# Attention states relative to each chunk's middle, with one decayed key and query, and forget gates of latents and context as 512-column products

## The chip, the cores and the metric

The kernel runs on one core of a Trainium2 chip. The metric is the time of one execution on the device in microseconds; lower is better. The core's engines are TensorE (PE, with its loads of stationary operands as PEld), VectorE (DVE), ScalarE (ACT), GpSimd (POOL) and SyncE (SP, which issues most DMAs). Each takes its instructions in program order and waits on semaphores for the others.

## The reference

One block over 256 latent tokens with 256 context tokens, width 1024: modulated norm, one combined projection, two mixers (a bidirectional gated linear recurrence in chunks of 64 with a state from the context, and a spatial MLP), projections and gates, and then a mixture of 32 experts. The change is in the recurrence and the projections of its forget gates.

```python
def decay(f_logit, lb):
    f = lb + (1.0 - lb) * jax.nn.sigmoid(f_logit.astype(jnp.float32))
    return heads(1.0 - f), heads(jnp.log(f))
...
def step(s, xs):                       # one chunk of 64 tokens, per head and direction
    qc, kc, vc, gc = xs
    b = jnp.cumsum(gc, axis=1)
    b_ref = b[:, A_CHUNK // 2 - 1:A_CHUNK // 2]
    b_end = b[:, -1]
    scores = jnp.einsum('bthd,bshd->bhts', qc * jnp.exp(b - b_ref), kc * jnp.exp(b_ref - b))
    scores = jnp.where(lower, scores, 0.0)
    o = (jnp.einsum('bhts,bshv->bthv', scores, vc)
         + jnp.einsum('bthd,bhdv->bthv', qc * jnp.exp(b), s))
    s = (jnp.exp(b_end)[..., None] * s
         + jnp.einsum('bshd,bshv->bhdv', kc * jnp.exp(b_end[:, None] - b), vc))
    return s, o
...
def final_state(k, v, logf):           # over the context, gives the first s
    tail = lax.cumsum(logf, axis=1, reverse=True) - logf
    return jnp.einsum('bshd,bshv->bhdv', k * jnp.exp(tail), v)
```

## The kernel before

Every dense product is computed as three products of rounded parts: `split` (L263) has ACT round a tile to `hi` and DVE subtract to get `lo`, for the weights as `ghi` and `glo`, for the modulated activations as `hh` and `hl`. A `Granule` is 1024 x 256 weights, fetched by SP into a ring of three slots; `dense` (L330) goes over it in two halves of four k-tiles, each with its own `ghi` and `glo`.

Phase one: the modulation weights and the modulated activations come in four quarters, together with pair 0's values and forget gates (24 to 84 us). Then a loop over j = 0 to 4 with eight heads in pairs. Iteration j computes the dense projections of pair j (`pair_dense`: d0 values, d1 query, d2 output gate, d3 and d4 the two forget gates; in iteration 4 gates of the second mixer instead) and the attention of the pair before: for its two heads x and y step 0 is `decays`, 1 `states`, 2 `output`, 3 `finish`. The string `ORDER` (L1056) gives the order in which the program is written, "x0 d0 y0 m0 d1 x1 m1 d2 x2 y1 x3 m2 d3 y2 m3 y3 d4"; a scheduler then orders each engine's instructions. m0 to m3 are parts of the weighted sums of later modulation weights: POOL multiplies 128x2048 (L215), adds halves (L216, L221); DVE does the other part (L228). In the profile pairs 1 to 4 stand at 84 to 157, 157 to 228, 228 to 298 and 298 to 345 us (the iteration in which their attention is done for the pair before).

`decays` takes the sigmoid of both forget gates (k, latents and context side by side): DVE maps it to f (L442), ACT takes the logarithm, POOL makes 1 - f (L446). DVE's scans (L453) run along tokens, per chunk in the latents (bl) and over the whole context (cu), per direction. d1 is bl relative to the chunk's middle (L466), d2 the chunk's end relative to bl (L467). Five exponentials on ACT follow, and five products: on DVE q and k for the scores (L475, L476), k for the states (L477), q for the output (L479), and on POOL the context's k (L478).

`states`: scores on PE (L496), k transposed (L506) and copied by ACT or DVE (L507), the chunks' state updates U and the context's state (L515, L518; in banks `ua` and `ub`). `output`: per direction three steps S[next] = S * decay of the chunk + U on DVE (L528, L530), then o on PE (L535, L539). `finish` normalises and gates.

After the loop: the second mixer, gates, branch projections, `w_out`, the router (345 to about 500 us), and the experts, whose 12 MB each are fetched through slots made of whatever phase one no longer needs (`slots`, L774 and after), the tags d0 to d3 and big1 of the pool `consts` among them.

Of the kernel before, what the change touches and what calls it, by code (L numbers as in the profile page):

```python
# [31 lines left out]
def kernel(  # L32
# [406 lines left out]
    def decays(hd, k, q):  # L439

        for dr in range(2):
            ve.tensor_scalar(k[:, dr], k[:, dr], omlb[dr][:, hd:hd + 1], lb[dr][:, hd:hd + 1], op0=OP.mult, op1=OP.add)  # L442
# [2 lines left out]
        tc.keep_in_program_order(sc.activation(lf, k, AF.Ln))
        gp.tensor_scalar(k, k, -1.0, 1.0, op0=OP.mult, op1=OP.add)  # L446
# [3 lines left out]
        def scan(o, dst, src, so, m, rev):  # L450
            st = -1 if rev else 1
            e = T - 1 if rev else 0
            ve.tensor_tensor_scan(view(dst, o + e, [[st, T]]), m, view(src, so + e, [[st, T]]),  # L453
                                  0.0, op0=OP.mult, op1=OP.add)

        chunks, whole = reset, view(reset, 1, [[0, T]])
        scan(0, bl, lf, 0, chunks, False)
        scan(T, bl, lf, 2 * T, chunks, True)
        scan(0, cu, lf, T, whole, True)
        scan(T, cu, lf, 3 * T, whole, False)  # L460
# [631 lines left out]
```

## Time and profile before

| what | value |
|---|---|
| median of 3 runs | 1448.78 us (1447.9 to 1449.63) |
| profiled execution: own time, span of its trace | 1449.62 us, 1447.4 us |
| granted clock of PE, mean | 0.98 |
| busy share of the span: PE, DVE, ACT, POOL | 93%, 44%, 21%, 11% |
| DMA | 487.41 MB, mean 337 GB/s |

The shares are means over stages that differ: the first third is phase one, the rest the experts. Matmuls are pipelined, and a row's duration is longer than the step to the next one; the pitch of a stretch is its length over its matmuls. An idle time in brackets names what ended it.

### The profile page before, as it was taken

The page shows a single profiled execution, that of the slowest core. Times are in us where ns is not written, and L with a number is a line of the kernel's source. Part 1 is how long each engine was busy: PE and PEld are TensorE (multiplying, and loading weights), DVE is VectorE, ACT ScalarE, POOL GpSimd, SP SyncE. Part 2 cuts the span into 40 slices and gives each one's busy share as a digit, 9 for nine tenths or more (in the row PEclk, how much of TensorE's full clock was granted, in tenths as well). Part 3 has the DMA queues.
Part 4 walks back from the last instruction along what each step waited for, and adds up shares of the span by engine and source line. Part 5 has one row for each costly group of instructions (what it writes and reads, how often), then busy time and mean ns, then how long its engine had stood idle before and what let it go on. Part 6 is the DMA issues. An engine that isn't in the chain of part 4 may idle for free. (4 is left out here: it accounts for less than half of the span.)

```text
span 1447.4 us, 19272 instructions
## 1 busy us (share of the span) xinstructions
PE 1344.3 (93%) x8190; PEld 750.8 (52%) x8190; DVE 643.5 (44%) x1106; ACT 307.7 (21%) x493; POOL 161.6 (11%) x107
## 2 busy tenths in 40 slices
PE   6979898989999999999999999989999899999996
PEld 4979788878999843333333333323333233232322
DVE  5498888888769623223223222222232232322214
ACT  2363444454444310100100101000000000000001
POOL 3054323240046000000000000000000000000001
PEclk8989999999999999999999999999999999999999
DMA  9535252534894899999999999999999999999994
GB/s 334 189 116 196 96 198 67 203 117 155 287 263 173 315 422 392 423 425 424 423 426 425 426 422 423 426 428 422 425 424 424 426 426 424 423 425 426 425 424 183
DMA packets 109909, 487.41 MB, mean 337 GB/s; under 512 B 6614, under 2 KB 65115, under 8 KB 77435
## 3 DMA queue, kind: packets, MB, share of 16 engines
q1 hardware_dynamic: 108970, 483.38, 83.5%
q0 software_dynamic: 848, 2.75, 0.6%
q8 instruction: 66, 1.08, 0.3%
q14 instruction: 25, 0.20, 0.0%
HBM read 485.06 MB, written 1.05 MB: 336 GB/s over the span
## 5 line engine op out<-in xcount | busy, mean ns | idle before, releaser
L829 PE MATMUL gate<-w,xT 128*64 128x512 f32 x1024 | 270.9, 608 | 18.5 <-DMA w<-in_w_dram 18.1
L829 PE MATMUL lin<-w,xT 128*64 128x512 f32 x1024 | 264.0, 594 | 0.0
L866 PE MATMUL py<-w,hT 128*64 128x512 f32 x992 | 223.1, 595 | 22.1 <-DMA w<-in_w_dram 22.0
L885 DVE SCALAR_TENSOR_TENSOR acc<-sc,wts,acc 128x512 f32<-128x512 f32 x122 | 86.0, 747 | 214.0 <-PE sc L882 214.0
L345 PE MATMUL acc<-hh,ghi 128*128 128x256 f32 x576 | 167.5, 291 | 11.5 <-ACT iv L427 11.5
L345 PE MATMUL acc<-hh,glo 128*128 128x256 f32 x576 | 165.8, 288 | 10.3 <-DVE glo L266 10.3
L345 PE MATMUL acc<-hl,ghi 128*128 128x256 f32 x576 | 165.3, 287 | 0.0
L266 DVE TENSOR_TENSOR glo<-w,ghi 128x1024 fp32r<-128x1024 f32 (+1 forms) x99 | 141.8, 1439 | 49.7 <-ACT ghi L265 49.3
L829 PEld LDWEIGHTS lin<-w,xT 128*64 128x64 f32 x1024 | 73.5, 138 | 147.9 <-issue 147.9
L866 PEld LDWEIGHTS py<-w,hT 128*64 128x64 f32 x992 | 69.1, 136 | 156.0 <-issue 111.7
L829 PEld LDWEIGHTS gate<-w,xT 128*64 128x64 f32 x1024 | 63.1, 137 | 158.2 <-issue 104.9
L265 ACT ACTIVATE ghi<-w 128x1024 fp32r<-128x1024 f32 (+1 forms) x102 | 102.3, 1007 | 144.7 <-PE acc L345 110.1
L345 PEld LDWEIGHTS acc<-hh,ghi 128*128 128x128 f32 x576 | 111.4, 193 | 12.7 <-ACT iv L427 11.9
L345 PEld LDWEIGHTS acc<-hh,glo 128*128 128x128 f32 x576 | 111.1, 193 | 11.7 <-DVE glo L266 11.5
L345 PEld LDWEIGHTS acc<-hl,ghi 128*128 128x128 f32 x576 | 111.5, 194 | 0.7 <-issue 0.7
L869 DVE TENSOR_TENSOR y<-py,g2h 128x512 f32<-128x512 f32 x31 | 21.4, 692 | 183.9 <-PE py L866 183.9
L964 POOL DMA_DIRECT2D bc<-in_final_g_dram x1 | 0.6, 557 | 892.4 <-DMA w<-in_w_dram 892.4
L804 ACT ACTIVATE xT<-misc,sh,a 128x128 f32<-128x128 f32 (+1 forms) x68 | 30.7, 452 | 284.3 <-DVE xT L806 284.3
L806 DVE TENSOR_SCALAR xT<-misc,a,sh 128x128 f32<-128x128 f32 (+1 forms) x68 | 27.3, 401 | 136.0 <-PE misc L800 125.4
L345 PE MATMUL acc<-ghi,hh 128*128 128x256 f32 x256 | 73.9, 291 | 13.7 <-DVE og L416 6.3
L836 DVE TENSOR_SCALAR g<-gate 128x512 f32<-128x512 f32 x32 | 22.1, 692 | 137.2 <-PE gate L829 137.2
L800 PEld LDWEIGHTS misc<-p,acc 128*128 128x128 f32 x544 | 66.6, 196 | 26.6 <-issue 26.0
(325 smaller groups left out, 1696.9 us busy)
## 6 DMA issues: line engine op xcount, KB each, us to landing
w<-in_w_dram SPq DMA_DIRECT2D x127, 2048.0 KB, 27.1
w<-in_w_dram SPq DMA_DIRECT2D x130, 1024.0 KB, 27.1
w<-in_w_in_dram SPq DMA_DIRECT2D x33, 1024.0 KB, 5.5
w<-in_w_mod_dram SPq DMA_DIRECT2D x24, 1024.0 KB, 5.6
w<-in_w_branch_b_dram SPq DMA_DIRECT2D x4, 1024.0 KB
w<-in_w_branch_a_dram SPq DMA_DIRECT2D x4, 1024.0 KB, 12.7
w<-in_w_out_dram SPq DMA_DIRECT2D x4, 1024.0 KB, 10.6
w<-in_w_in_dram SPq DMA_DIRECT2D x12, 256.0 KB, 8.6
```

Of the source, the lines that this page charges most:

```text
L265: sc.activation(hi, src, AF.Copy)
L266: eng.tensor_sub(lo, src, hi)
L345: te.matmul(o, l, r, start=opens and kt == 0 and n == 0, stop=kt == KT - 1 and n == 2, skip_group_check=True)
L800: te.matmul(pg[:, k], view(x1, tt * D + kt // 2 * 256 + kt % 2, [[2, P]]), tok[:, tt], start=tt == 0, stop=tt == 1)
L804: sc.activation(xT[:, kt], pg[:, k], AF.Identity, bias=sh2[:, kt:kt + 1], scale=a2[:, kt:kt + 1])
L806: ve.tensor_scalar(xT[:, kt], pg[:, k], a2[:, kt:kt + 1], sh2[:, kt:kt + 1], op0=OP.mult, op1=OP.add)
L829: te.matmul(zz[n][h * C:(h + 1) * C], xT[:, kt], w[:, 0, n * D + h * 512:n * D + (h + 1) * 512], start=False, stop=kt == KT - 1, skip_grou ...
L836: ve.tensor_scalar(g, zz[0], 7.0, None, op0=OP.min)
L866: te.matmul(py[h * C:(h + 1) * C], hT2[:, kt % 4, (kt // 4) * C:(kt // 4) * C + C], w[:, k, h * 512:(h + 1) * 512], start=False, stop=kt = ...
L869: ve.tensor_mul(y, py, g2h)
L885: ve.scalar_tensor_tensor(acc[:, tt, s], pcs[h], wcol[tt], old[:, tt, s], op0=OP.mult, op1=OP.add)
L964: gp.dma_start(fgbc, bcast(final_g, D))
```

## The change

The states are kept relative to the middle of each chunk. The key for the scores, k * exp(b_ref - b), is then also that of the state updates, and the query q * exp(b - b_ref) also that of the output; d2, two exponentials, and two DVE products a head are left out. What remains of the decays are factors per chunk and channel: `w` (128x16), copied on POOL from bl and d1 and exponentiated. A step of the state is an addition (S + U) and a scaling by two such factors, on DVE for one direction and on POOL for the other; the context's state is scaled when ACT copies it.

The logarithm takes scale and bias, so that L442 goes (ACT's logarithm is four 128x512 of two heads instead of two 128x1024); products with 1 - f become scalar_tensor_tensor with the negated factor; POOL's 1 - f covers the context alone; the scan over the context starts one token late with a memset column instead of a subtraction on POOL (L462).

Latents and context lie side by side in one buffer (`both`), and a forget granule is 48 products of 512 columns instead of 96 of 256. The two buffers take the whole tags d2 and d3 (two units each), so the experts' slots are d0, d1 and big1 with one unit, d2 and d3 with two, and two instead of three in `ringc`.

```diff
-    hT = [(consts.tile([P, KT, T], F32R, name="hh0", tag="d3"), consts.tile([P, KT, T], F32R, name="hl0", tag="d2")),
-          (mid.tile([P, KT, T], F32R, name="hh1"), mid.tile([P, KT, T], F32R, name="hl1"))]
+    both = (consts.tile([P, KT, 2, T], F32R, name="hh", tag="d3"), consts.tile([P, KT, 2, T], F32R, name="hl", tag="d2"))
+    hT = [[t[:, :, a] for t in both] for a in range(2)]
+    both = [t.rearrange("p k a t -> p k (a t)") for t in both]
...
-        return [(pps[ct][:, a], ct, hT[a], a == 0) for ct in range(2) for a in range(2)]
+        return [(pps[ct].rearrange("p a t -> p (a t)"), ct, both, True) for ct in range(2)]
...
-        for dr in range(2):
-            ve.tensor_scalar(k[:, dr], k[:, dr], omlb[dr][:, hd:hd + 1], lb[dr][:, hd:hd + 1], op0=OP.mult, op1=OP.add)
...
-        tc.keep_in_program_order(sc.activation(lf, k, AF.Ln))
-        gp.tensor_scalar(k, k, -1.0, 1.0, op0=OP.mult, op1=OP.add)
+        for dr in range(2):
+            tc.keep_in_program_order(sc.activation(lf[:, dr], k[:, dr], AF.Ln, scale=omlb[dr][:, col], bias=lb[dr][:, col]))
+        kl, kc = k[:, :, 0:T], k[:, :, T:2 * T]
+        gp.tensor_scalar(kc, kc, -1.0, None, op0=OP.add)
...
+        gp.memset(view(cu, T - 1, [[1, 2]]), 0.0)
...
-        gp.tensor_sub(cu, cu, e2)
...
-        ve.tensor_sub(view(d2, 0, [[T, 2], [64, 4], [1, 64]]), view(bl, 63, [[T - 63, 2], [64, 4], [0, 64]]), bl4)
+        w = wk.tile([P, 2, 2, 4], F32, name="w")
+        gp.tensor_copy(w[:, 0], view(bl, 31, [[T + 1, 2], [64, 4]]))
+        gp.tensor_copy(w[:, 1], view(d1, 63, [[T - 63, 2], [64, 4]]))
         sc.activation(e1, d1, AF.Exp)
         sc.activation(e2, d1, AF.Exp, scale=-1.0)
-        sc.activation(bl, bl, AF.Exp)
-        sc.activation(d2, d2, AF.Exp)
         sc.activation(cu, cu, AF.Exp)
-        qb = q[:, None, :].to_broadcast([P, 2, T])
-        kl, kc = k[:, :, 0:T], k[:, :, T:2 * T]
-        ve.tensor_mul(e1, e1, qb)
-        ve.tensor_mul(e2, e2, kl)
-        ve.tensor_mul(d2, d2, kl)
+        sc.activation(w, w, AF.Exp)
+        for dr in range(2):
+            ve.scalar_tensor_tensor(e1[:, dr], e1[:, dr], nomlb[dr][:, col], q, op0=OP.mult, op1=OP.mult)
+        ve.scalar_tensor_tensor(e2, kl, -1.0, e2, op0=OP.add, op1=OP.mult)
         gp.tensor_mul(cu, cu, kc)
-        ve.tensor_mul(d1, bl, qb)
-        return e1, e2, bl, d1, d2, cu
+        return e1, e2, cu, w
...
-            for a, src in ((0, kb), (1, kc)):
+            for a, src in ((0, kt_), (1, kc)):
...
-            sc.activation(S[:, 0, 0], ua[:, 3], AF.Copy)
-            sc.activation(S[:, 1, 3], ub[:, 3], AF.Copy)
+            sc.activation(S[:, 0, 0], ua[:, 3], AF.Copy, scale=w[:, 0, 0, 0:1])
+            sc.activation(S[:, 1, 3], ub[:, 3], AF.Copy, scale=w[:, 0, 1, 3:4])
             for n in range(3):
-                m = 3 - n
-                ve.scalar_tensor_tensor(S[:, 0, n + 1], S[:, 0, n], eb[:, 0, n * 64 + 63:n * 64 + 64], U[0, n],
-                                        op0=OP.mult, op1=OP.add)
-                ve.scalar_tensor_tensor(S[:, 1, m - 1], S[:, 1, m], eb[:, 1, m * 64:m * 64 + 1], U[1, m],
-                                        op0=OP.mult, op1=OP.add)
+                for dr, a, b in ((0, n, n + 1), (1, 3 - n, 2 - n)):
+                    r = R[:, dr, b]
+                    ve.tensor_add(r, S[:, dr, a], U[dr, a])
+                    (gp if dr else ve).tensor_scalar(S[:, dr, b], r, w[:, 1, dr, a:a + 1], w[:, 0, dr, b:b + 1],
+                                                     op0=OP.mult, op1=OP.mult)
...
-                        te.matmul(o[cc * 64:cc * 64 + 64, tt], qh[:, dr, ch * 64:ch * 64 + 64], S[:, dr, ch],
+                        te.matmul(o[cc * 64:cc * 64 + 64, tt], qt[:, dr, ch * 64:ch * 64 + 64], S[:, dr, ch],
...
-    slots += [(consts, f"d{i}", 1) for i in range(4)] + [(consts, "big1", 1)] + [(ringc, "w", 2)] * RING_C
+    slots += [(consts, t, n) for t, n in (("d0", 1), ("d1", 1), ("big1", 1), ("d2", 2), ("d3", 2))] + [(ringc, "w", 2)] * RING_C
...
-RING_C = 3
+RING_C = 2
```

The order of instructions changes too. ACT in pair 3, before, from the logarithms of both heads (names end in a number of the tile; cu is the context's decay, iv the values of the next pair):

```order
L445 ACTIVATE lf_2477<-sg0_1736 128x1024
L445 ACTIVATE lf_2614<-sg1_1737 128x1024
L468 ACTIVATE lf_2477<-d1_2488 128x2x256
L265 ACTIVATE ghi_2675<-w_2644 128x1024
L470 ACTIVATE bl_2481<-bl_2481 128x512
L471 ACTIVATE d2_2489<-d2_2489 128x512
L427 COPY iv_2470<-acc_2502 128x512
```

and in the changed kernel (its L450 is the logarithm, of which two rows of four are shown, L472 to L474 the exponentials, L431 the copy of iv):

```order
L450 ACTIVATE lf_2205<-sg0_1554,lba0_711,lbb0_712 128x512
L450 ACTIVATE lf_2340<-sg1_1555,lba0_711,lbb0_712 128x512
L474 ACTIVATE cu_2211<-cu_2211 128x512
L472 ACTIVATE lf_2205<-d1_2217 128x2x256
L473 ACTIVATE lf_2205<-d1_2217 128x2x256
L265 ACTIVATE ghi_2401<-w_2370 128x1024
L474 ACTIVATE cu_2346<-cu_2346 128x512
L472 ACTIVATE lf_2340<-d1_2352 128x2x256
L473 ACTIVATE lf_2340<-d1_2352 128x2x256
L431 COPY iv_2200<-acc_2230 128x512
```

The first copy of iv stood behind three exponentials of one head, and stands now behind six of two.

POOL from pair 2's output to pair 3's decays, before (ks holds the states):

```order
L478 TENSOR_TENSOR cu_1882<-cu_1882,sg1_1006 128x512
L215 TENSOR_TENSOR w_2639<-w_2639,cs32_163 128x2048
L216 TENSOR_TENSOR w_2639<-w_2639 128x1024
L221 TENSOR_TENSOR modrow_2468<-w_2639 128x512
L215 TENSOR_TENSOR w_2915<-w_2915,cs32_163 128x2048
L446 TENSOR_SCALAR sg0_1736<-sg0_1736 128x1024
L216 TENSOR_TENSOR w_2915<-w_2915 128x1024
L446 TENSOR_SCALAR sg1_1737<-sg1_1737 128x1024
L462 TENSOR_TENSOR cu_2482<-cu_2482,lf_2477 128x512
```

and in the changed kernel (L530 scales states, L452 is 1 - f for the context, L470 copies into w):

```order
L530 TENSOR_SCALAR ks_1799<-ks_1799,w_1570 128x128 x3
L455 MEMSET cu_2346 128x2
L215 TENSOR_TENSOR w_2365<-w_2365,cs32_163 128x2048
L216 TENSOR_TENSOR w_2365<-w_2365 128x1024
L221 TENSOR_TENSOR modrow_2198<-w_2365 128x512
L530 TENSOR_SCALAR ks_1941<-ks_1941,w_1705 128x128 x3
L215 TENSOR_TENSOR w_2647<-w_2647,cs32_163 128x2048
L452 TENSOR_SCALAR sg0_1554<-sg0_1554 128x2x256
L216 TENSOR_TENSOR w_2647<-w_2647 128x1024
L470 COPY w_2219<-bl_2210 128x8
```

The scalings of the second head's states (ks_1941) stand behind L215, L216 and L221 of the modulation weights w_2365, those of the first head (ks_1799) ahead of them.

DVE in pair 3 before, from the last L442:

```order
L266 TENSOR_TENSOR glo_2648<-w_2644,ghi_2647 128x1024
L442 TENSOR_SCALAR sg1_1737<-sg1_1737,lbb1_822,lba1_821 128x512
L453 SCALAR_TENSOR_TENSOR bl_2481<-attc_119,lf_2477 128x256 x2
L453 SCALAR_TENSOR_TENSOR cu_2482<-attc_119,lf_2477 128x256 x2
L466 TENSOR_TENSOR d1_2488<-bl_2481 128x512
L467 TENSOR_TENSOR d2_2489<-bl_2481 128x512
```

and now, without L442 and without d2 between the two heads' scans (L458 scans, L467 d1, L477 the query, L478 the key), up to the second half of the weights of the step d1 (glo_2402), which stands behind head x's key; rows of the same kind on the same tiles are left out:

```order
L266 TENSOR_TENSOR glo_2374<-w_2370,ghi_2373 128x1024
L458 SCALAR_TENSOR_TENSOR bl_2210<-attc_119,lf_2205 128x256
L458 SCALAR_TENSOR_TENSOR cu_2211<-attc_119,lf_2205 128x255
L467 TENSOR_TENSOR d1_2217<-bl_2210 128x512
L458 SCALAR_TENSOR_TENSOR bl_2345<-attc_119,lf_2340 128x256
L458 SCALAR_TENSOR_TENSOR cu_2346<-attc_119,lf_2340 128x255
L467 TENSOR_TENSOR d1_2352<-bl_2345 128x512
L477 SCALAR_TENSOR_TENSOR lf_2205<-lf_2205,lbn0_722,q_1552 128x256
L478 SCALAR_TENSOR_TENSOR lf_2205<-sg0_1554,lf_2205 128x2x256
L266 TENSOR_TENSOR glo_2402<-w_2370,ghi_2401 128x1024
```

On PE thirteen of the sixteen score products of head x stood behind all of d1's 48 products and stand now ahead of the first, so that d1 follows head x's key.

## Rows read from the trace of the kernel before

**Rows 1.** Windows of the span: bounds and length (us), then each engine's busy us with its instructions (PEld is the load of stationary operands), PE's granted clock as a share of full speed, DMA share and GB/s.
```profile
24.00:84.00 60.00, 60.00 (x531) 55.20 (x532) 34.05 (x63) 24.95 (x38) 10.43 (x8) 0.97 0.65 206
84.00:157.00 73.00, 64.14 (x571) 60.33 (x570) 64.33 (x105) 35.46 (x53) 28.24 (x14) 0.93 0.51 168
298.00:345.00 47.00, 38.91 (x355) 36.66 (x353) 42.76 (x47) 29.61 (x38) 18.35 (x9) 0.93 0.42 139
345.00:500.00 155.00, 154.59 (x1295) 151.39 (x1294) 111.78 (x154) 68.47 (x99) 41.01 (x28) 1.00 0.73 238
560.00:1420.00 860.00, 819.35 (x3886) 291.85 (x3884) 227.85 (x403) 63.05 (x117) 0.56 (x1) 1.00 1.01 424
```

**Rows 2.** Timeline of PE, the rows at which it had been idle for a stretch or more than a microsecond in pairs 1 to 4: start, duration, instruction; in brackets the idle time before it and what ended it.
```profile
86.77 0.36 PE L345 MATMUL acc<-ghi,hh 128*128 128x256 f32 x1 [1.17 <-DVE q L416]
100.65 0.55 PE L345 MATMUL acc<-ghi,hh 128*128 128x256 f32 x1 [6.35 <-DVE og L416]
174.71 0.58 PE L345 MATMUL acc<-hh,ghi 128*128 128x256 f32 x1 [5.55 <-ACT iv L427]
246.21 0.58 PE L345 MATMUL acc<-hh,ghi 128*128 128x256 f32 x1 [5.96 <-ACT iv L427]
317.70 0.58 PE L345 MATMUL acc<-hh,glo 128*128 128x256 f32 x1 [6.66 <-DVE glo L266]
```

**Rows 3.** Windows of PE directly after three of these rows; columns as in the first group.
```profile
100.65:106.70 6.05, 6.05 (x29) 0.51 0.00 0
174.71:178.29 3.58, 3.58 (x17) 0.50 0.00 0
246.21:249.99 3.78, 3.78 (x18) 0.50 0.00 0
```

**Rows 4.** Window of PE, instructions of L345 alone (256 columns), in a stretch of gates and branch projections without a hole.
```profile
405.30:430.30 25.00, 25.00 (x209) 25.00 (x210) 1.00 0.83 243
```

**Rows 5.** Timeline of ACT before PE's restart in pair 3.
```profile
245.07 0.61 ACT L471 ACTIVATE d<-d 128x512 f32<-128x512 f32 x1
245.59 0.57 ACT L427 COPY iv<-acc 128x512 f32<-128x512 f32 x1
```

**Rows 6.** Timeline of DVE: pair 1 (81), pair 3 (231 to 246), the output of the second head of pair 3 (278), pair 4 (304).
```profile
81.83 3.06 DVE L442 TENSOR_SCALAR sg<-sg,lbb,lba 128x512 f32<-128x512 f32 x2
230.97 0.54 DVE L442 TENSOR_SCALAR sg<-sg,lbb,lba 128x512 f32<-128x512 f32 x1
232.69 5.44 DVE L453 TENSOR_TENSOR_SCAN bl<-attc,lf 128x256 f32<-128x256 f32 x2 [1.18 <-ACT lf L445]
238.05 4.19 DVE L453 TENSOR_TENSOR_SCAN cu<-attc,lf 128x256 f32<-128x256 f32 x2
244.42 1.26 DVE L453 TENSOR_TENSOR_SCAN bl<-attc,lf 128x256 f32<-128x256 f32 x2
245.61 1.24 DVE L453 TENSOR_TENSOR_SCAN cu<-attc,lf 128x256 f32<-128x256 f32 x2
278.35 0.34 DVE L528 SCALAR_TENSOR_TENSOR ks<-ks,bl,ua 128x128 f32<-128x128 f32 x1
304.01 3.84 DVE L442 TENSOR_SCALAR sg<-sg,lbb,lba 128x512 f32<-128x512 f32 x1
```

**Rows 7.** Timeline of POOL: pair 3's modulation weights (232), and the next ones (274 to 281).
```profile
232.59 3.61 POOL L215 TENSOR_TENSOR w<-w,cs 128x2048 f32<-128x2048 f32 x1 [22.44 <-DMA w<-in_w_mod_dram]
274.16 3.61 POOL L215 TENSOR_TENSOR w<-w,cs 128x2048 f32<-128x2048 f32 x1 [16.98 <-DVE nt L107]
277.85 2.37 POOL L216 TENSOR_TENSOR w<-w 128x1024 f32<-128x1024 f32 x1
280.30 1.29 POOL L221 TENSOR_TENSOR modrow<-w 128x512 f32<-128x512 f32 x1
```

**Rows 8.** Timeline of PE in the experts, 512 columns: four products a row.
```profile
559.14 1.03 PE L829 MATMUL gate<-w,xT 128*64 128x512 f32 x4
560.00 1.02 PE L829 MATMUL lin<-w,xT 128*64 128x512 f32 x4
```

**Rows 9.** Groups of instructions over 60 to 345 us, shapes kept apart: busy us, mean ns of one, then idle time before them and its releaser.
```profile
L442 DVE TENSOR_SCALAR sg<-sg,lbb,lba 128x512 f32<-128x512 f32 x16 | 15.3, 966 | 2.3 <-ACT sg L436 2.3
L467 DVE TENSOR_TENSOR d<-bl 128x512 f32<-128x512 f32 x8 | 12.8, 1596 | 0.0
L477 DVE TENSOR_TENSOR d<-d,sg 128x512 f32<-128x512 f32 x8 | 5.4, 679 | 0.0
L479 DVE TENSOR_TENSOR d<-bl,q 128x512 f32<-128x512 f32 x8 | 5.4, 678 | 0.0
L462 POOL TENSOR_TENSOR cu<-cu,lf 128x512 f32<-128x512 f32 x8 | 13.1, 1641 | 18.0 <-DVE cu L453 18.0
L446 POOL TENSOR_SCALAR sg<-sg 128x1024 f32<-128x1024 f32 x8 | 11.7, 1468 | 1.5 <-ACT lf L445 1.5
```

**Rows 10.** Window of pair 3 behind PE's restart.
```profile
246.20:262.40 16.20, 12.59 (x112) 11.70 (x112) 16.20 (x18) 9.62 (x15) 6.58 (x4) 0.88 0.42 140
```

**Rows 11.** Window of the experts' second stretch.
```profile
540.00:560.00 20.00, 20.00 (x108) 8.76 (x108) 6.09 (x14) 3.06 (x6) 0.00 (x0) 1.00 0.89 360
```

**Rows 12.** Timeline of SP's DMA queue before the first expert (issues of several DMAs are one row: start, time to the last issue's end, count).
```profile
476.35 15.19 SPq L73 DMA_DIRECT2D w<-in_w_dram  x8
497.41 0.33 SPq L69 DMA_DIRECT2D w<-in_w_dram  x1
```

More of the change, by code (lines that the diff above doesn't have):

```diff
@@ L387 @@
     gncol = cols2[:, 40:41]
-    lb, omlb = [], []
+    lb, omlb, nomlb = [], [], []
     for k in range(2):
@@ L404 @@
         omlb.append(eb)
+        ng = late.tile([P, 8], F32, name=f"lbn{k}")
+        ve.tensor_scalar(ng, ea, 1.0, -1.0, op0=OP.mult, op1=OP.add)
+        nomlb.append(ng)
     early.close()
@@ L439, in decays @@
     def decays(hd, k, q):
[L441 to L442 removed]
+        col = slice(hd, hd + 1)
         lf = wk.tile([P, 2, 2 * T], F32, name="lf")
         tc.keep_in_program_order(sc.preload_act_table_set("natural_log_exp_and_others"))
[L445 to L446 removed]
+        for dr in range(2):
+            tc.keep_in_program_order(sc.activation(lf[:, dr], k[:, dr], AF.Ln, scale=omlb[dr][:, col], bias=lb[dr][:, col]))
@@ L447, in decays @@
+        kl, kc = k[:, :, 0:T], k[:, :, T:2 * T]
+        gp.tensor_scalar(kc, kc, -1.0, None, op0=OP.add)
         bl = wk.tile([P, 2, T], F32, name="bl")
         cu = wk.tile([P, 2, T], F32, name="cu")
[L450 to L460, printed above, removed]
+        gp.memset(view(cu, T - 1, [[1, 2]]), 0.0)
+        def scan(dst, o, src, so, m, n, st):
+            ve.tensor_tensor_scan(view(dst, o, [[st, n]]), m, view(src, so, [[st, n]]), 0.0, op0=OP.mult, op1=OP.add)
+        whole = view(reset, 1, [[0, T - 1]])
+        scan(bl, 0, lf, 0, reset, T, 1)
+        scan(bl, 2 * T - 1, lf, 3 * T - 1, reset, T, -1)
@@ L461, in decays @@
+        scan(cu, T - 2, lf, 2 * T - 1, whole, T - 1, -1)
+        scan(cu, T + 1, lf, 3 * T, whole, T - 1, 1)
         e1, e2 = lf[:, :, 0:T], lf[:, :, T:2 * T]
-        gp.tensor_sub(cu, cu, e2)
         d1 = wk.tile([P, 2, T], F32, name="d1")
-        d2 = wk.tile([P, 2, T], F32, name="d2")
-        bl4 = view(bl, 0, [[T, 2], [64, 4], [1, 64]])
-        ve.tensor_sub(view(d1, 0, [[T, 2], [64, 4], [1, 64]]), bl4, view(bl, 31, [[T + 1, 2], [64, 4], [0, 64]]))
-        ve.tensor_sub(view(d2, 0, [[T, 2], [64, 4], [1, 64]]), view(bl, 63, [[T - 63, 2], [64, 4], [0, 64]]), bl4)
+        ve.tensor_sub(view(d1, 0, [[T, 2], [64, 4], [1, 64]]), view(bl, 0, [[T, 2], [64, 4], [1, 64]]),
+                      view(bl, 31, [[T + 1, 2], [64, 4], [0, 64]]))
@@ L488, in states @@
         def states():
-            qt, kt_, eb, qh, kb, kc = dec
+            qt, kt_, kc, w = dec
             for dr in range(2):
@@ L518, in states @@
                     te.matmul(bk[:, 3], kn[:, 1, 2 * dr + tt], iv[:, 2 + tt, vs], start=tt == 0, stop=tt == 1)
-            st.update(sm=sm, S=S, U=U, ua=ua, ub=ub)
+            st.update(sm=sm, S=S, R=kn, U=U, ua=ua, ub=ub)
         def output():
-            eb, qh = dec[2:4]
-            sm, S, U, ua, ub = (st[k] for k in ("sm", "S", "U", "ua", "ub"))
-            sc.activation(S[:, 0, 0], ua[:, 3], AF.Copy)
-            sc.activation(S[:, 1, 3], ub[:, 3], AF.Copy)
+            qt, w = dec[0], dec[3]
+            sm, S, R, U, ua, ub = (st[k] for k in ("sm", "S", "R", "U", "ua", "ub"))
+            sc.activation(S[:, 0, 0], ua[:, 3], AF.Copy, scale=w[:, 0, 0, 0:1])
+            sc.activation(S[:, 1, 3], ub[:, 3], AF.Copy, scale=w[:, 0, 1, 3:4])
             for n in range(3):
-                m = 3 - n
-                ve.scalar_tensor_tensor(S[:, 0, n + 1], S[:, 0, n], eb[:, 0, n * 64 + 63:n * 64 + 64], U[0, n],
-                                        op0=OP.mult, op1=OP.add)
-                ve.scalar_tensor_tensor(S[:, 1, m - 1], S[:, 1, m], eb[:, 1, m * 64:m * 64 + 1], U[1, m],
-                                        op0=OP.mult, op1=OP.add)
+                for dr, a, b in ((0, n, n + 1), (1, 3 - n, 2 - n)):
[3 more added lines that the diff above has]
+                                                     op0=OP.mult, op1=OP.mult)
             o = bank("o_ps", (P, 2, P))
@@ L645 @@
         ve.tensor_scalar(v[:, tt], v[:, tt], mv[:, tt, 0:1], rs[:, tt:tt + 1], op0=OP.subtract, op1=OP.mult)
-    ybh = mid.tile([P, KT, T], F32R, name="hh1")
-    ybl = mid.tile([P, KT, T], F32R, name="hl1")
+    ybh, ybl = hT[1]
     for j in range(4):
@@ L691 @@
     gp.dma_start(acc, x[0].rearrange("(t p) d -> p t d", p=P))
-    mhi = mid.tile([P, KT, T], F32R, name="hh1")
-    mlo = mid.tile([P, KT, T], F32R, name="hl1")
+    mhi, mlo = hT[1]
     for j in range(4):
```

## The prediction

> **What bounds the kernel now.** I read the stages first, by windows of the span [rows 1]. From 560 to 1420 us the experts' weights arrive at 424 GB/s without a break, so nothing that makes that stretch's compute cheaper shortens it; it starts when the phase before it lets it. From 345 to 500 us TensorE (PE) is busy 154.59 of 155 us, with work that this change hardly touches. The four attention pairs lie between 84 and 345 us, and there neither PE nor DMA is full: in the first it works 64.14 of 73 us, in the last 38.91 of 47, while VectorE (DVE) has 64.33 and 42.76 us of work. So phase one is PE-bound with holes, and a hole filled or a product saved moves all that follows.
>
> Next the timeline of PE, for the holes and what ended them [rows 2]. Each pair has one large hole: 6.35 us until DVE had finished og, 5.55 and 5.96 us until ScalarE (ACT) had copied iv, 6.66 us until DVE had written glo. With the small one at 86.77 that is 25.7 us. After three of them PE runs 64 products in 13.41 us at a granted clock of 0.50 or 0.51 [rows 3], the 1.2 GHz level; at the pitch of a full-clock stretch, 25.00 / 209 = 0.1196 us [rows 4], they would take 7.65, so 5.8 us more go there.
>
> Then the releasers. The iv copy at 245.59 is 0.57 us long and was not waiting for PE: it stands in ACT's queue behind the exponentials of head x [rows 5], and those wait for DVE. DVE in that pair goes scans, differences, scans [rows 6]: two scans of 128x256 take 5.44 us and the next two 4.19, where the same pairs at 244.42 take 1.26. GpSimd (POOL) explains it: L215 runs from 232.59 for 3.61 us [rows 7], and L446 and L216 follow it. DVE instructions whose operands all lie in SBUF wait until POOL's instruction is over, and the reverse.
>
> **The change, part by part.** *Forget products.* In pairs 1 to 3 two granules of 96 products of 256 columns become 48 of 512. Four 512-column products take 0.86 us, 559.14 to 560.00 [rows 8]: 0.215 each against 2 x 0.1196 = 0.239. 48 x 0.024 = 1.16 us a granule, six granules: **-7.0**. Bounds: 0 if float products of this kind pair worse than the expert products that I take the row from, -7.0 otherwise. The same two granules of pair 0 (2.3 us) lie in the start, where PE is busy 60.00 of 60 us [rows 1]; but the latents' half of these products used to be work for PE while the context was being modulated, and now waits for it. I take **-1**, between -2.3 and +3.
>
> *Key, query and decays.* Over 60 to 345 us DVE loses L442 (15.3 us), L467 (12.8), L477 and L479 (5.4 each), 38.9 us; POOL loses L462 (13.1) and half of L446's 11.7 [rows 9]. ACT's two exponentials of bl and d2 go, and a 128x16 one comes. Most of this lies beside PE's products; only what stands ahead of a hole counts.
>
> Pair 1: ahead of og's product stand L442 (81.83, two in 3.06 us [rows 6]) and an L467 (1.6 in the mean [rows 9]), 4.7 us. The e2 product of head x (about 0.7) moves ahead of it: **-4** of 6.35. Bounds 0 (the scans inherit the wait for POOL from L442) and -6.35.
>
> Pair 3: L442 at 230.97 (0.54) and two halves of L446 (1.4) go from in front of the scans of x, and an L467 (1.6) from between x and y. The scans of y end at 246.8 now; with a d1 of 0.7 (what L477 takes for as many elements) they and d1 of y are then done at about 246.8 - 0.5 - 1.4 - 1.6 + 0.7 = 244.0. But in the new order of ACT the iv copy stands behind the exponentials of both heads, six of about 0.6 [rows 5], not behind three of x: the last three start after 244.0, so the copy comes at about 244.0 + 1.8 = 245.8 and ends at 246.4. PE's restart stays where it is, 246.2 to 247. After it PE idles 16.20 - 12.59 = 3.6 us in the next 16 while DVE is busy 16.20 of 16.20 [rows 10]; there DVE loses 1.6 (L467 of y) and four products of 0.68 (L477, L479), 4.3 us, so most of these waits go: **-2** net. Pair 2 has the same order and hole: **-2**. Bounds for each: +3 (PE now has the scores of x ahead of d1, so it waits for e2 of x as well) and -9.6 (both the hole and the small waits go).
>
> Pair 4: L442 at 304.01 lasts 3.84 us because L215 is running; without it the first scan waits for the same L215, so that gain is small, but an L467 goes from ahead of the glo that ends the hole (1.6), and again with the second head: **-4** of the 6.66 and what follows. Bounds -1 and -8.
>
> *Output chain.* Six DVE instructions a head (L528 and L530, 0.34 us, one every 0.25: 278.35) become six additions and three scalings on DVE and three scalings on POOL. Without waits DVE spends 3 x 0.25 = 0.8 us more a head. PE has dense products to run beside it. What is new is POOL's queue: the scalings of head y stand behind L215, L216 and L221 of the next modulation weights, which run 274.16 to 281.6 [rows 7], while the old chain of that head started at 278.35. So that chain may begin 3.3 us late. I expose 1 us in each of three pairs: **+3**; bounds +0 and +10 (3.3 in three pairs).
>
> The Trainium skill, SBUF — State Buffer, Who interferes with whom, says that a DVE instruction with at most one SBUF input outside the two-port modes never meets GpSimd, and that a scaling from SBUF to SBUF can take a two-port mode and then locks or is locked out for a whole instruction. The row at 278.35 agrees for the old chain (0.34 beside L216, one operand in PSUM), the row at 304.01 for a scaling (3.84). By that rule the three new DVE scalings could each wait for a POOL instruction, +10 in place of +3.
>
> *Expert slots.* The same number of units; d2 and d3 become free when w_out's last product reads the second half of the buffer instead of earlier. Eight issues of 1 MB stand at 476 to 491 us, the next at 497.41 [rows 12]; two of the eight now go out near 497, so DMA may stand for 0 to 1.5 us; but at 540 to 560 us it runs at 360 GB/s because the slots are full [rows 11], so what is lost before is made up there: **0**, bounds -1 and +1.5.
>
> **Sum.** -7 - 1 - 4 - 2 - 2 - 4 + 3 = -17 us. Against the profiled execution's 1449.62 (0.84 above the median of the three runs) that is 1432.6; against the median 1431.8. I say 1432.
>
> **Rivals.** *The holes go altogether* (15%): DVE is relieved by 10 us a pair, more than each hole. For it: with 10 us less DVE would no longer end any hole. Against: the scans, which stay, and POOL's L215 and L216, which stay, are the longest things in the chain. 25.7 + 5.8 + 3.6 = 35.1 us in the holes, the slow products and pair 3's small waits, 8 of products, and 3 back for the output chain: -35.1 - 8 + 3 = -40 at most, around -32 with a third of the holes left: 1409 to 1418.
> *Only the products gain* (20%): the waits move, to e2 of x ahead of d1 and the iv copy behind both heads (+3 in pairs 2 and 3), and pair 1's and 4's gain goes to scans that wait for L215. -7 - 1 - 2 + 6 - 2 + 3 = -3 to -8: 1441 to 1446.
> *Slower* (8%): the output chain of head y is locked out by POOL. Its price is up to 7.3 us a head (3.61 + 2.37 + 1.29 [rows 7]) if PE has no product left in front of the o_ps product; it decides from 17 / 3 = 5.7 us exposed in each of three pairs, and then the time is 1449 to 1456. Against: in the old order the chain of head y was at most 3.3 us ahead of the end of L221.
> *Wide products cost what two narrow ones do* (7%): 0.239 each; then -17 + 8 = -9: 1440.
>
> **Numbers.** The forecast itself has half of the chance (its own range 1424 to 1440). Holding 8 in 10: 1416 to 1445, which leaves out the slower case, the far end of the first rival and that of the second. A measurement of this kernel can tell about 0.2%, 2.9 us: faster 0.86, same 0.07, slower 0.07.
>
> **What would show it.** In the new profile the forget products are 512 columns wide at 0.215 us; no DVE instruction stands in L442's place; the restart of PE after pair 3's hole lies within 2 us of the end of the exponentials of y and is released by the iv copy; the small waits of the 16 us behind it are under 1.5 us; DVE's busy time in 84 to 345 us falls by 30 us or more; the hole of pair 1 is 2 to 3 us. Wrong: a wait of PE of over 3 us on ks, S or POOL's L530; DMA under 400 GB/s at 490 to 510 us; or DVE's chain as long as before, because the scans take L442's waits.

## The result and the profile after

The changed kernel takes 1437.89 us in the median (1435.19 to 1439.14, 4 runs) where the kernel before takes 1448.34 beside it: a ratio of 0.9915 (0.9894 to 0.9936), about -10.5 us, clear of no change. The forecast was 1432 (1416 to 1445). The profiled execution took 1439.14 us, its span 1437.4.

The experts took no part. Their first product stands 9.8 us earlier, at 499.33 us instead of 509.11, and from there to the end of the span it is 938.3 and 938.1 us. The row in PE's timeline, of the kernel before:

```profile
509.11 0.65 PE L829 MATMUL gate<-w,xT 128*64 128x512 f32 x2
```

and of the changed one:

```profile
499.33 0.65 PE L827 MATMUL gate<-w,xT 128*64 128x512 f32 x2
```

So the whole gain lies in phase one. A landmark in both traces is the last sigmoid of a pair's forget gates on ACT (L436, now L440), at 73.2, 158.6, 229.7 and 302.7 us before and 73.8, 160.2, 227.6 and 300.0 after. From one to the next (and from the last to the first expert):

| stretch | before | after | difference | forecast |
|---|---|---|---|---|
| start | 73.2 | 73.8 | +0.6 | -1 |
| pair 1 | 85.4 | 86.4 | +1.0 | -5.3 |
| pair 2 | 71.1 | 67.4 | -3.7 | -3.3 |
| pair 3 | 73.0 | 72.4 | -0.6 | -3.3 |
| pair 4 and the rest of phase one | 206.4 | 199.3 | -7.1 | -4 |
| experts | 938.3 | 938.1 | -0.2 | 0 |

(The forecast of a pair is its term, a third of the -7.0 of the products, and 1 us for the output chain.)

The windows that answer [rows 1] show PE still with holes in the pairs (second and third line; the first is the start), and DVE with 5 to 7 us less of work in each pair. From 84 to 345 us DVE's busy time goes from 224.2 to 202.3 us, 21.9 less; the prediction's sign was 30 or more:

```profile
24.00:84.00 60.00, 56.98 (x424) 47.54 (x424) 34.94 (x68) 25.70 (x41) 9.99 (x11) 0.97 0.64 203
84.00:157.00 73.00, 65.81 (x475) 56.42 (x476) 57.68 (x94) 33.55 (x51) 30.52 (x22) 0.93 0.52 174
298.00:345.00 47.00, 42.97 (x389) 39.42 (x388) 37.73 (x64) 30.15 (x44) 19.53 (x15) 0.93 0.45 152
```

And PE's holes of a microsecond and more, with the one at og (97.42), which answer [rows 2]:

```profile
84.53 0.39 PE L346 MATMUL acc<-hh,glo 128*128 128x256 f32 x1 [3.48 <-DVE glo L266]
90.40 0.36 PE L346 MATMUL acc<-ghi,hh 128*128 128x256 f32 x1 [1.03 <-DVE q L420]
97.42 0.36 PE L346 MATMUL acc<-ghi,hh 128*128 128x256 f32 x1 [0.98 <-DVE og L420]
115.77 1.17 PE L518 MATMUL ua<-iv,ks 128*128 128x128 f32 x4 [1.99 <-ACT ks L507]
138.60 0.50 PE L556 MATMUL tp<-ident,on 128*128 128x128 f32 x2 [2.65 <-DVE on L553]
176.53 0.64 PE L496 MATMUL scores<-lf 128*32 128x64 f32 x10 [6.03 <-DVE lf L478]
244.69 0.85 PE L496 MATMUL scores<-lf 128*32 128x64 f32 x26 [6.97 <-DVE lf L478]
275.85 0.50 PE L556 MATMUL tp<-ident,on 128*128 128x128 f32 x2 [2.39 <-DVE on L553]
311.40 0.58 PE L346 MATMUL acc<-hh,glo 128*128 128x256 f32 x1 [3.77 <-DVE glo L266]
```

The hole of pair 1 at og has shrunk from 6.35 to 0.98 us, that of pair 4 from 6.66 to 3.77, and the small waits behind the holes of pairs 2 and 3 have vanished. But those two holes have grown to 6.03 and 6.97 us, and three new ones of 2.4 to 3.5 us and one of 1.99 stand where there were none. (The kernel before had three more of 1.3 to 1.4 us, at 91.44, 262.49 and 326.60, which [rows 2] leaves out.)

What DVE did ahead of these holes (first fence, DVE's timeline), and what POOL did at the same moment (second):

```profile
79.32 4.03 DVE L467 TENSOR_TENSOR d<-bl 128x512 f32<-128x512 f32 x1
86.26 3.40 DVE L266 TENSOR_TENSOR glo<-w,ghi 128x1024 fp32r<-128x1024 f32 x1
130.09 2.81 DVE L103 TENSOR_SCALAR nv<-ss 128x2 f32<-128x2 f32 x1
230.33 2.62 DVE L458 TENSOR_TENSOR_SCAN bl<-attc,lf 128x256 f32<-128x256 f32 x1 [1.39 <-ACT lf L450]
234.41 2.82 DVE L458 TENSOR_TENSOR_SCAN cu<-attc,lf 128x255 f32<-128x255 f32 x1
267.98 3.56 DVE L108 SCALAR_TENSOR_TENSOR nt<-nt,nv 128x2 f32<-128x2 f32 x1
```

```profile
79.15 3.65 POOL L215 TENSOR_TENSOR w<-w,cs 128x2048 f32<-128x2048 f32 x1
85.75 2.83 POOL L216 TENSOR_TENSOR w<-w 128x1024 f32<-128x1024 f32 x1
129.26 3.62 POOL L215 TENSOR_TENSOR w<-w,cs 128x2048 f32<-128x2048 f32 x1 [4.48 <-ACT junk L548]
228.58 3.83 POOL L215 TENSOR_TENSOR w<-w,cs 128x2048 f32<-128x2048 f32 x1 [17.22 <-DMA w<-in_w_mod_dram]
234.22 2.46 POOL L216 TENSOR_TENSOR w<-w 128x1024 f32<-128x1024 f32 x1
267.92 3.61 POOL L215 TENSOR_TENSOR w<-w,cs 128x2048 f32<-128x2048 f32 x1 [0.77 <-DMA w<-in_w_mod_dram]
```

Each long DVE row ends with POOL's row, or later by what it takes when it is free: L103, on two elements, at 132.90 against POOL's 132.88; L108 at 271.54 against 271.53; L467 of 128x512 at 83.35 against 82.80, 0.55 us later (it takes 0.66 when free, at 94.88); the first scan at 232.95 against 232.41. DVE has less to do, but what it still does meets the same three POOL instructions of the modulation sums.

PE's idle time is only half of the story. From pair 0's last gate to the first expert product it goes from 36.8 to 31.2 us, 5.6 less, and PE's busy time from 399.1 to 394.3, 4.8 less. The last stretch of the table, all engines as in [rows 1], of the kernel before and of the changed one:

```profile
302.74:509.11 206.37, 197.18 (x1667) 189.43 (x1665) 160.05 (x236) 98.58 (x139) 59.36 (x37) 0.98 0.67 225
300.02:499.33 199.31, 193.65 (x1669) 185.70 (x1667) 148.70 (x237) 97.58 (x139) 60.28 (x45) 0.98 0.69 232
```

Half of its 7.1 us is busy time, though no forget product stands there and PE does the same work. The products of 256 columns follow each other faster. One window among the gates and branch projections, dense products alone, of the kernel before, of wide_only (below; the attention of before with the new buffer) and of the changed kernel:

```profile
405.80:430.80 25.00, 25.00 (x211) 25.00 (x210) 1.00 0.84 244
405.80:430.80 25.00, 25.00 (x211) 24.86 (x210) 1.00 0.79 237
405.80:430.80 25.00, 25.00 (x221) 25.00 (x221) 1.00 0.78 226
```

Behind pair 4's last gate the mean step between two such products at the full clock is 119.2 ns before and 115.8 after. It is 118.8 to 119.2 in the four kernels of this document with the old attention and 115.3 to 116.7 in the ten with the new one, whatever the width of the forget products. So it came with the new attention; by what in it, no run here shows. Some 1260 steps of 3.4 ns less are 4.3 us (an estimate from these rows), and nothing in the forecast stands for them.

### The profile page after: what moved, and what is told of

Read it like the earlier page. It is cut to its first block, busy times and chain, and to the rows that moved or that the text cites. A ratio compares the mean times of both kernels' runs of the same rounds, so it can differ in the third digit from the quotient of the medians.

```text
span 1437.4 us, 18504 instructions
## 1 busy us (share of the span) xinstructions
PE 1341.1 (93%) x7806; PEld 727.7 (51%) x7806; DVE 615.9 (43%) x1100; ACT 306.2 (21%) x494; POOL 171.8 (12%) x147
## 5 line engine op out<-in xcount | busy, mean ns | idle before, releaser
L864 PE MATMUL py<-w,hT 128*64 128x512 f32 x992 | 227.2, 605 | 26.0 <-DMA w<-in_w_dram 25.9
L346 PE MATMUL acc<-hh,glo 128*128 128x256 f32 (+1 forms) x480 | 150.1, 314 | 7.3 <-DVE glo L266 7.3
L266 DVE TENSOR_TENSOR glo<-w,ghi 128x1024 fp32r<-128x1024 f32 (+1 forms) x99 | 130.4, 1321 | 50.0 <-ACT ghi L265 49.7
L346 PE MATMUL acc<-hh,ghi 128*128 128x256 f32 (+1 forms) x480 | 151.6, 316 | 0.0
L346 PE MATMUL acc<-hl,ghi 128*128 128x256 f32 (+1 forms) x480 | 149.8, 312 | 0.0
L346 PEld LDWEIGHTS acc<-hh,glo 128*128 128x128 f32 x480 | 95.1, 198 | 12.3 <-DVE glo L266 7.8
L346 PEld LDWEIGHTS acc<-hh,ghi 128*128 128x128 f32 x480 | 94.9, 198 | 4.5 <-issue 0.8
L346 PEld LDWEIGHTS acc<-hl,ghi 128*128 128x128 f32 x480 | 94.9, 198 | 4.2 <-issue 0.4
L835 ACT ACTIVATE s<-g 128x512 f32<-128x512 f32 x32 | 20.2, 630 | 282.7 <-DVE g L834 282.7
```

The costliest lines, as they stand in the source:

```text
L266: eng.tensor_sub(lo, src, hi)
L346: te.matmul(o, l, r, start=opens and kt == 0 and n == 0, stop=kt == KT - 1 and n == 2, skip_group_check=True)
L835: sc.activation(s, g, AF.Sigmoid, scale=1.702)
L864: te.matmul(py[h * C:(h + 1) * C], hT2[:, kt % 4, (kt // 4) * C:(kt // 4) * C + C], w[:, k, h * 512:(h + 1) * 512], start=False, stop=kt = ...
```

## Experiments

Beside each group of runs the kernel before ran too, at 1449.6 to 1450.8 us in the median; ratios are against it, differences in microseconds are between medians. The changed kernel was not run again with them; its 1437.89 us was measured beside a kernel before of 1448.34, so differences against it are good to some 2 us. "Theory" below is that DVE's waits for POOL's part of the modulation sums (L215, L216, L221) took back what the change had gained; the rivals are the new order (scores of x ahead of d1, the iv copy behind both heads) and products that are no cheaper wide.

**narrow.** The forget products back to 256 columns.

```diff
-        return [(pps[ct].rearrange("p a t -> p (a t)"), ct, both, True) for ct in range(2)]
+        return [(pps[ct][:, a], ct, hT[a], a == 0) for ct in range(2) for a in range(2)]
```

> The changed kernel with its forget products back at 256 columns (96 a granule, one buffer as in the changed kernel); all else as changed. If 48 wide products cost 1.16 us a granule less than 96 narrow ones, the six granules of pairs 1 to 3 bring back 7 us and pair 0 at most 2 more: 1445 to 1447 us. If wide products cost what two narrow ones do: 1438. If the narrow latents' products are useful fill while the context is modulated, pair 0 gains up to 3 and the sum is 1442 to 1443.

Measured: 1438.1 us, ratio 0.991 (0.9892 to 0.9929), the same as the changed kernel. Nothing comes back that these runs can tell: the second of the three numbers. Yet a wide product does not cost quite what two narrow ones do. One window of PE in the forget products ahead of pair 4, of the changed kernel and of this run:

```profile
288.31:295.63 7.32, 7.32 (x33) 6.01 (x32) 1.00 0.43 143
286.64:294.06 7.42, 7.42 (x64) 7.42 (x64) 1.00 0.44 137
```

In the first, 32 products pass from the first start to the last, 7.32 / 32 = 0.2287 us each; in the second 63 narrow ones, 0.1178 each, 0.2356 for two. The kernel before has 0.1188 at this place (7.96 us for 67 steps from 290.18), 0.2376 for two. The row from which the forecast was made had 0.215 [rows 8]: it has a stationary operand of 64 columns (128*64), the forget products one of 128. So a granule saves 48 x 0.0069 = 0.33 us against this run and 0.43 against the kernel before, 2.0 and 2.6 us in six granules, not 7. Two microseconds are too few to show in these medians.

**narrow_start.** Only pair 0 back to narrow products (the start's call of `four_outs` with a third argument False).

```diff
-            dense(g, four_outs(pps, natural), natural, ((2 * q, 2),), ve if q else gp)
+            dense(g, four_outs(pps, natural, False), natural, ((2 * q, 2),), ve if q else gp)
```

> The changed kernel with pair 0's forget products at 256 columns (latents apart from context, as before) and those of pairs 1 to 3 at 512. In the run with all products narrow the start ended 2.3 us earlier (last sigmoid at 71.5 against 73.8 us), since the latents' products fill PE's waits for the context. Theory: the start loses 2 us by the wide products; this kernel stands 2 to 3 us below the changed one, near 1435. Rival: pair 1 bound by DVE and POOL swallows it: 1437 to 1438.

Measured: 1437.43 us, 0.9908 (0.9887 to 0.9928): no difference that the runs can tell. The start itself is shorter: from PE's first product with modulated activations (at about 23 us) to pair 0's last sigmoid it takes 50.4 to 51.5 us in the five kernels whose start is wide and 48.3 to 49.8 in the nine whose start is narrow, the kernel before among them: 1.9 us between the means, but in this run's own profile only 0.7 (49.8 against 50.4). The rival named pair 1, yet pair 1 is shorter too in this profile (83.7 us against 86.3); pair 2 loses it again (71.1 against 67.4).

**wide_only.** The other way round: the attention of before with the wide products, the one buffer and the new slots.

> The kernel before with the one buffer, the 512-column forget products and the new list of expert slots, and with its attention as it was. By the sum of the prediction -7 in pairs 1 to 3, -1 in the start and 0 for the slots: 1440 to 1441 us. If the start loses by the missing fill: 1442 to 1444. If the holes of the pairs swallow what the products save: 1446 or more.

Measured: 1447.16 us, 0.9974 (0.9959 to 0.9989), -3.6 us. That is the last of the three numbers. Its own wide products take 0.2324 us (41 steps from 287.66), which against 0.2376 gives 0.25 us a granule, 1.5 in pairs 1 to 3, just under the interval (1.6 to 5.9). The profile of it also shows pairs 1 and 2 with other holes than before, so the rest can't be put down to one cause here.

**no_pool_mods** and **before_no_pool_mods.** In both kernels POOL's half of the sums is left out, DVE's stays.

```diff
-                gp.tensor_mul(wt, wt, cs32[:, 4 * k4:4 * k4 + 4, 0:1].to_broadcast([P, 4, 512]))
-                gp.tensor_add(wt[:, 0:2], wt[:, 0:2], wt[:, 2:4])
...
+                gp.tensor_add(wt[:, 0, 0:8], wt[:, 0, 0:8], wt[:, 1, 0:8])
...
-                    if kt == 0:
+                    if kt == 4:
```

> The changed kernel with POOL's half of the modulation sums left out (L215, L216 and L221 become one tiny addition; the sums then lack that half, DVE's half stays). Theory: what is left of the holes of pairs 1 to 4 is DVE waiting for these POOL instructions at every turn (L467 4.03 us in pair 1, scans of 2.6 and 2.8 in pair 3, two-element instructions of 2.8 and 3.6 in the norm). Then the holes of 3.5, 2.7, 6, 7, 2.4 and 3.8 us shrink to less than half: 1420 to 1427 us. Rival: the holes come from the new order (scores of x ahead of d1, iv copy behind both heads); then at most 3 us: 1435 to 1438.

> The kernel before with the same half of the modulation sums left out. If POOL's turns are what kept the change from its full 17 us, then the two kernels without them stand 15 to 20 us apart, and this one comes at 1438 to 1443. If the turns cost both the same, they stand 10 apart as with them: 1432 to 1436.

Measured: 1414.39 us for the changed kernel, 0.975 (0.9727 to 0.9773), and 1432.55 for the one before, 0.9871 (0.9851 to 0.9891). The theory, not the rival, and by more than its number: with the same order of DVE's instructions and the same one ending them, holes of 6 and 7 us become 3.06 and 2.91. What remains, about 3 us a pair, is what the new order has PE wait for, the key of x; so the rival is not nothing. POOL's sums cost the old kernel 18 us and the changed one 23.5. Without them the change is worth 18 us, within the 15 to 20 expected; both kernels came out 5 to 6 us below their ranges, and the old one alone lies at the number of its rival (1432 to 1436). It is the distance that speaks for the theory.

**dve_mods** and **before_dve_mods.** Nothing left out: POOL's half of the sums goes to DVE, in each of eight sums one instruction of 0.48 us and three of 0.77 in place of POOL's three.

```diff
-MOD_POOL = (0,)
+MOD_POOL = ()
```

> The changed kernel with POOL's half of the modulation sums moved to DVE (MOD_POOL empty: four instructions of 0.75 us in place of L215, L216 and L221), so that nothing is left out. Theory: a turn costs more than the work, as POOL's 7.3 us a sum come in front of single DVE instructions; DVE gets 3 us more of work a sum, 24 in all, of which little lies on the chain: 1420 to 1428 us. Rival: what is added on DVE delays the chain as much as POOL's turns did: 1435 to 1442.

> The kernel before with POOL's half of the modulation sums on DVE. If POOL's turns are what the change lost its gain to, then without them the change is worth its sum again: this kernel stands 17 to 25 us above the changed one with the same sums on DVE (1409.6), at 1426 to 1435. If the change is worth 10 to 12 with and without turns: 1419 to 1422. If the old kernel's DVE has no room for 24 us more work: above 1435.

Measured: 1409.59 us, 0.9715 (0.9692 to 0.9739), 10 below the theory's number, and 1433.77, 0.9887 (0.9867 to 0.9907), within it. DVE takes on more work and all is faster; between the two kernels the change is now worth 24 us instead of 10. Since its pairs stand earlier, the windows go from gate to gate here. Pairs 1 and 3 of the changed kernel:

```profile
73.82:160.16 86.34, 76.21 (x557) 66.16 (x557) 67.33 (x103) 41.03 (x61) 37.15 (x25) 0.94 0.51 170
227.58:300.02 72.44, 63.08 (x479) 55.57 (x478) 54.44 (x91) 29.64 (x52) 27.14 (x22) 0.93 0.39 131
```

and of dve_mods, with PE nearly full and a granted clock of 1.00 (2.4 GHz, where 0.93 is a mean with stretches at 1.2, as 0.50 from 244.69 to 249.00):

```profile
73.65:148.35 74.70, 71.34 (x557) 61.72 (x556) 59.70 (x114) 42.38 (x61) 17.46 (x16) 1.00 0.58 190
210.97:272.25 61.28, 59.08 (x479) 52.23 (x478) 47.53 (x99) 29.37 (x51) 11.97 (x16) 1.00 0.48 155
```

DVE's busy time is 7 us shorter in each (59.70 against 67.33, 47.53 against 54.44) though it does more, since a busy time includes the wait for POOL. The groups of the scans over 60 to 345 us, (busy us, mean ns of one, idle before them), of the changed kernel:

```profile
L458 DVE TENSOR_TENSOR_SCAN bl<-attc,lf 128x256 f32<-128x256 f32 x16 | 20.0, 1248 | 8.0 <-ACT lf L450 8.0
L458 DVE TENSOR_TENSOR_SCAN cu<-attc,lf 128x255 f32<-128x255 f32 x16 | 16.9, 1059 | 0.0
```

and of dve_mods:

```profile
L458 DVE TENSOR_TENSOR_SCAN bl<-attc,lf 128x256 f32<-128x256 f32 x16 | 13.4, 839 | 1.0 <-ACT lf L450 1.0
L458 DVE TENSOR_TENSOR_SCAN cu<-attc,lf 128x255 f32<-128x255 f32 x16 | 11.3, 705 | 0.0
```

And PE's holes at the places of 176.53 and 244.69, which the iv copy ends now as it did before the change:

```profile
161.91 0.39 PE L346 MATMUL acc<-hh,ghi 128*128 128x256 f32 x1 [2.84 <-ACT iv L431]
223.30 0.38 PE L346 MATMUL acc<-hh,ghi 128*128 128x256 f32 x1 [2.20 <-ACT iv L431]
```

**order_late.** narrow_start with the sums still on POOL but later in the program.

```diff
-ORDER = "x0 d0 y0 m0 d1 x1 m1 d2 x2 y1 x3 m2 d3 y2 m3 y3 d4"
+ORDER = "x0 d0 y0 d1 m0 x1 d2 m1 x2 y1 x3 d3 y2 m2 y3 m3 d4"
```

> Like narrow_start, and the sums stay on POOL but come later in the program: ORDER is x0 d0 y0 d1 m0 x1 d2 m1 x2 y1 x3 d3 y2 m2 y3 m3 d4, so that L215, L216 and L221 stand behind both heads' decays, and those of m2 among the second head's state steps. Theory: the scans, differences and products of the decays run without turns, pairs 1 to 3 gain 3 to 5 us each: 1421 to 1428 us. Rival: the sums meet the norm and the state steps instead, and as much is lost there: 1433 to 1440.

Measured: 1434.16 us, 0.9891 (0.987 to 0.9911), 3 us below narrow_start: the rival's number. The first holes of pairs 2 and 3 fall to 3.43 and 4.29 us, and others come in the norm (3.03 us until DVE's L555) and in pair 4. The pairs do gain: the last gate of pair 4 stands at 289.4 us against 300.1. But from there to the first expert it takes 204.2 us instead of 198.5.

**states_dve** and **dve_ns_states.** All state scalings on DVE, in the changed kernel and in dve_mods with a narrow start.

```diff
-                    (gp if dr else ve).tensor_scalar(S[:, dr, b], r, w[:, 1, dr, a:a + 1], w[:, 0, dr, b:b + 1],
+                    ve.tensor_scalar(S[:, dr, b], r, w[:, 1, dr, a:a + 1], w[:, 0, dr, b:b + 1],
```

> The changed kernel with all six scalings of a head's states on DVE, none on POOL. If POOL's scalings stand in the way (in POOL's queue behind L215, L216 and L221, or one step after the other between the engines), 3 to 6 us come back: 1432 to 1435. By the rule that a scaling from SBUF to SBUF on DVE can be locked out by POOL it would be 2 to 6 slower: 1440 to 1444. I expect neither: the chain runs beside PE's products, 1437 to 1439.

> The changed kernel with the sums on DVE, the start narrow and all state scalings on DVE: every part at its better place so far. If the steps between DVE and POOL cost what the run with the scalings on DVE showed (about 4 us): 1401 to 1405. If that came from other turns that are gone now: 1405 to 1409.

Measured: 1432.93 us, 0.9875 (0.9854 to 0.9897), 5 us below the changed kernel, the first of its numbers and not the one that I expected; and 1419.15, 0.9789 (0.9772 to 0.9805), 10 us above dve_ns and above both of its ranges. The signs contradict each other, so no price of the scalings follows. In the second the pairs end earlier than in dve_ns (last gate of pair 4 at 299.7 us against 308.1), and the loss lies behind them, where PE has 16 router products and a wait of 2.44 us for ACT ahead of the second mixer's products: the scheduler wrote the end of phase one in another order. (The profiled execution, 1414.03 us, is the fastest of five; it shows some 6 of the 10 us.)

**dve_ns** and **dve_narrow.** dve_mods with a narrow start, and with all forget products narrow.

> The changed kernel with the sums on DVE and pair 0's forget products narrow. With the holes of pair 1 nearly gone the start's 2 us should now reach the end: 1405 to 1408 us. If the start still doesn't count: 1409 to 1411.

> As the run before it, with the forget products of pairs 1 to 3 narrow too. PE is now without large holes, so what 48 wide products save shows: at the 0.2287 us of the changed kernel's trace against 2 x 0.1196 it is 0.5 us a granule, 3 us in six; at the predicted 0.215 it would be 7. So 3 above the run with a narrow start by the one, 7 by the other.

Measured: 1409.17 us, 0.9718 (0.9702 to 0.9735), the second of its ranges, and 1408.52, 0.9714 (0.9695 to 0.9732). The 7 us of the forecast are excluded. The pitches of these two traces, 0.229 against twice 0.1177, would give 2 us and not the 3 expected; with intervals of some 2.5 us each that is neither shown nor excluded. dve_mods, dve_ns and dve_narrow are one time, 1409, and 41 us below the kernel before.

## Why the prediction came out as it did

The time lay in the range and the sign was right; the gain was 10.5 us instead of 17. That it came so near is in part luck: some 4 us of it are the faster step of the 256-column products, which the forecast had as unchanged. Without them the gain would be about 6 us, near the upper end of the range. By the steps:

- *That phase one moves the end, the experts nothing*: right, 938.3 and 938.1 us. DMA did not stand for the slots that come free later (433 GB/s from 490 to 510 us).
- *Forget products, -7.0*: the term was mis-sized. 0.2287 us a product instead of 0.215, against 0.2376 for the two that it replaces, gives -2.6. The row taken [rows 8] had a smaller stationary operand; a row of the same operand did not exist, and the lower bound of 0 was the warning.
- *Start, -1*: wrong in sign, inside its bounds (+0.6). That PE is busy 56.98 of 60 us instead of 60.00 in [rows 1]'s window has nothing to do with it: the 3.0 us are the hole that ends at 84.53, pair 1's. Up to 73 us PE shows next to no wait:

```profile
24.00:73.00 49.00, 48.92 (x355) 39.68 (x356) 25.06 (x59) 19.32 (x33) 3.36 (x7) 0.97 0.72 226
```

  That a wide start is some 2 us longer is what the fourteen profiles show; that the latents' products are missing as fill is not shown, and the totals don't show the 2 us.
- *Pair 1, -4*: failed. The lower bound came true, "the scans inherit the wait for POOL from L442", only that d1 (L467) and glo inherited it: 4.03 and 3.40 us. POOL's first sum stands at 79.15 to 88.6 us in the changed kernel, where d1 and two of the glo now run.
- *Pairs 2 and 3, -2 each*: the place was right, a hole ended by DVE's and ACT's chain of both heads, with the small waits behind it gone. ACT copies the first half of iv at 243.31, but PE waits for the key of x, which DVE ends at 244.63, as the second rival had it; ACT's row, and then DVE's, which is long by a POOL instruction once more (free: 0.68):

```profile
243.31 0.57 ACT L431 COPY iv<-acc 128x512 f32<-128x512 f32 x1
```

```profile
242.88 1.75 DVE L478 SCALAR_TENSOR_TENSOR lf<-sg,lf 128x512 f32<-128x512 f32 x1
```

  Pair 3 loses what it gained to a place I had not priced: the norm, where an instruction on two elements waits 3.56 us for L215, and the output chain and PE's transposes stand behind it (2.39 us, then a clock of 0.54 from 276.0 to 279.4). The wait itself is not new. The kernel before has it at the same norm, but PE had products to run meanwhile and lost 0.59 us; DVE's row and PE's:

```profile
274.30 3.49 DVE L109 SCALAR_TENSOR_TENSOR rs<-nt,ny 128x2 f32<-128x2 f32 x1
278.32 0.30 PE L556 MATMUL tp<-ident,on 128*128 128x128 f32 x1 [0.59 <-DVE on L553]
```

  Pair 1 has such a hole now too (2.81 us in L103, PE 2.65).
- *Pair 4, -4*: the hole is 3.77 instead of 6.66, and PE's idle time from the last gate on 3.5 us less: near the term. That the stretch shows -7.1 is the faster step of the products, for which no term stood.
- *Output chain, +3, behind POOL's queue*: not the way it went. POOL's scalings waited for DVE, not behind the sums (141.07 us: idle 4.38 until DVE's L529); DVE's scalings take 0.36 us in the mean of 22. What the Trainium skill says of scalings from SBUF to SBUF (SBUF — State Buffer, Who interferes with whom) shows in L103, a scaling on one SBUF input that ended with POOL's instruction, and in one L530 of 22: at 205.94 it took 0.63 us instead of 0.34, until L216 had ended at 206.49. No long POOL instruction ran beside the other 21.

The step that failed as a whole is "DVE is relieved": I took DVE's instructions away and left the ones that wait. A wait for POOL was treated as part of an instruction's duration, to vanish with it; it belongs to POOL's instruction, and the next DVE instruction in line takes it. So DVE's busy time fell by 21.9 us and not by the 38.9 that were counted; at what they take when free, 0.54 us for L442 and 0.66 for the others, the four groups would come to some 24 us (an estimate). The runs without POOL's sums show what the waits cost: there the change is worth 18 to 24 us. That this lies about the sum of -17 does not confirm its terms, since some 4 us of it are again the faster step (119.2 and 115.9 ns with the sums on DVE) and the products gave 2.6 at most instead of 7.

What stays open: what in the new attention makes the 256-column products follow each other faster, which part of the 2 to 3 us of the wide products reaches the end, and what the scalings on POOL cost.

## What to carry to other kernels

Where DVE and POOL both work on SBUF, take the wait out of the durations before summing: an instruction of 0.66 us that shows 4.03 will hand its 3.4 us to its neighbour when it is removed. Look at POOL's long instructions first; moving eight times 7 us of POOL's work to eight times 3 us of DVE's gave 28 us here, more than the change itself, and made the change worth twice as much. Take the pitch of a matmul from a row with the same stationary operand. And compare the pitch of products that the change does not touch before putting a whole gain down to its holes.
